# Spreading per-token factors over the partitions: a transpose of the stretched column in place of an fp32 matmul with the identity

## The chip, the cores and the metric

The kernel runs on one core of one Trainium2 chip, as one launch. The metric is the device time of that launch in microseconds. A profile is one execution, recorded with the start and length of every instruction. The engines are TensorE (PE; its weight loads are PEld), VectorE (DVE), ScalarE (ACT), GpSimd (POOL) and SyncE (SP, which issues most of the DMA transfers). Each runs its own queue in order; semaphores tie them together.

## The reference

A token sequence of 256 positions by 1024 features goes through two layers of a first block and one layer of a second, in fp32. What matters here is that every stage begins with, or contains, a norm: a factor per token that multiplies all features of that token.

```python
def rms_norm(x, g):
    x32 = x.astype(jnp.float32)
    y = x32 * lax.rsqrt(jnp.mean(x32 * x32, axis=-1, keepdims=True) + EPS)
    return (y * g.astype(jnp.float32)).astype(x.dtype)

for i in range(DEPTH):                     # first block, DEPTH = 2
    x = x + 0.5 * swiglu(rms_norm(x, g[0]), ...)
    h = rms_norm(x, g[1])
    m = even_mixer(h, ...) if i % 2 == 0 else mla_mixer(h, ...)
    x = x + m
    x = x + 0.5 * swiglu(rms_norm(x, g[2]), ...)
    x = x + per_layer_embedding(rms_norm(x, g[3]), p[i], ..., g[4])   # ends in a norm
# second block, one layer
u = rmsnorm(x, norm_mix) @ w_in            # attention, a state-space part, pooling
x = x + concatenate([y_attn, y_ssd, y_pool]) @ w_out
x = x + swiglu(rmsnorm(x, norm_ffn), ...)
return rmsnorm(x, norm_final)
```

The even mixer holds a gated recurrence whose output has a norm per token and head (4 heads). The state-space part needs, per head (6), the running sum of a decay along the tokens, both down the partitions and along the columns: `exp(a_cum[l] - a_cum[s])`; its output has a norm per token and group (2 groups).

## The kernel before

Activations lie feature-major: 128 features down the partitions, 256 tokens along the columns, eight such tiles for 1024 features. Weights stream in from HBM as pieces of 128 x 2048 and are split on chip into a high and a low part (`whi` by ACT at line 248, `wlo` by DVE at line 249), as are the activations (`hh` and `hl`, or `big`, or `o`). Each product of a 128 x 128 weight tile is three matmuls of 256 columns, high by high, high by low, low by high, which accumulate in a bank (`acc`, four of them). A second set of four banks (`aux`) takes everything small.

`fm` (line 319) runs a list of weight chunks over the eight (or 22) activation tiles; its evacuation multiplies by the factor per token `rb`. That factor is made beside the matmuls by `Stat`: `begin` (line 69) lets PE sum the squares into a column per half of the tokens, with the token on the partition, and DVE takes the reciprocal root; `finish` (line 88) then has to turn each column of 128 factors into a row that stands on all 128 partitions, since tokens lie along the columns in what it multiplies. The column is read with a stride of zero, as if it were 128 equal columns, and PE multiplies its transpose by the identity, into one half of an `aux` bank; ACT copies the bank to `rb` (line 99).

```python
for b in range(NB):                                   # NB = 2, line 92
    k.bcast(pb[:, b * P : (b + 1) * P], self.r[:, b : b + 1].to_broadcast([P, P]))
```

The same `bcast` (line 289) is used in the recurrence's output norm (line 808, eight times), in `states` of the state-space part (line 1293, two calls of six) and in `normed` (lines 1352 to 1354, six times; the middle one takes a column pair that was spread to 64 columns each, `kw`). Each goes through `mm` (line 162), the helper by which nearly all matmuls are issued, so the profile shows them under line 163, and they are told apart by their tiles: `ident` and `ny`, `ac` or `kw`.

The order on each engine is made by the framework's planner, which goes through the program with priorities and its own cost for every instruction and puts instructions that are ready into the queues. The kernel steers it: `behind(ins)` (line 165) holds what is issued inside it until `ins` has been placed, and `high_priority` lets DVE's and ACT's work of a norm go first. The ten calls of `finish` from within `fm` and the eight broadcasts of the recurrence's norm are behind a named matmul. The three calls through `now` (line 102: the two norms that close a layer embedding, and the last norm) and those of `states` and `normed` are not.

Where the kernel transposes data, as in `attend` (line 1119), in latent attention (`transposed`, line 936) and for the state-space inputs (line 1274), it uses `nc.tensor.transpose` with the same identity tile already.

Of the kernel before, what the change touches and what calls it, by code (L numbers as in the profile page):

```python
# [106 lines left out]
class Kern:  # L107
# [180 lines left out]

    def bcast(self, out, col, w=P):

        self.mm(out, col, self.ident)


    def sq_add(self, src, j, own=False):
# [1346 lines left out]
```

## Time and profile before

| | us |
|---|---|
| timed runs, median of 3 | 1368.15 |
| lowest and highest of them | 1366.81, 1370.12 |
| the profiled execution, its own time | 1364.73 |
| its span, first to last instruction | 1363.0 |
| PE busy | 1335.7 |
| DVE busy | 920.0 |
| ACT busy | 726.8 |

The span is what the views of the profile divide up; the profiled execution's own time is 1.7 us longer. A view by time merges neighbouring instructions of one kind on one engine into a row with a count; the second number is then the time from the first one's start to the last one's end. Matmuls overlap: each is listed with a length from its start until its last result, and the next starts long before that. The clock that the throttle granted to PE stands as a share of full speed (1.00 is 2.4 GHz, 0.50 is 1.2 GHz). A weight load and its matmul are two instructions (PEld and PE).

### The profile page before, as it was taken

What the parts mean: (1) busy time and instruction counts of PE and PEld (TensorE: products, weight loads), DVE (VectorE), ACT (ScalarE), POOL (GpSimd) and SP (SyncE); (2) the same over time, 40 slices, a digit from 0 to 9 for tenths busy, and PEclk for the clock granted to TensorE, in tenths of its full rate; (3) what the DMA queues carried; (4) which work ended last, traced back from release to release, by engine and by line L of the source; (5) the groups of instructions that cost most, each with busy time, mean ns of one, the idle gap of its engine ahead of it and who ended that gap; (6) DMA issues with size and microseconds to landing.
All of it is one profiled execution on the core that took longest, in us unless ns stands there. A gap on an engine that the chain in (4) does not pass through costs nothing.

```text
span 1363.0 us, 25969 instructions
## 1 busy us (share of the span) xinstructions
PE 1335.7 (98%) x10872; PEld 1304.9 (96%) x10872; DVE 920.0 (67%) x1527; ACT 726.8 (53%) x1110; POOL 78.3 (6%) x94
## 2 busy tenths in 40 slices
PE   8999999999999999999999899999998999999997
PEld 7999999999999999999999679999998988999997
DVE  6866657968666557866556767766558786766643
ACT  6554546646554456655445656544445665644442
POOL 3100010002000001000010002000001000200001
PEclk9999999999999999999999999999998999999998
DMA  9755555244555453555455323555554442555541
GB/s 323 244 185 183 171 201 173 90 174 168 200 188 203 160 203 138 200 190 188 166 194 193 108 90 132 184 188 188 180 185 156 155 149 100 181 190 187 185 158 60
DMA packets 34645, 235.50 MB, mean 173 GB/s; under 512 B 3984, under 2 KB 4496, under 8 KB 6880
## 3 DMA queue, kind: packets, MB, share of 16 engines
q1 hardware_dynamic: 32976, 230.24, 48.9%
q0 software_dynamic: 832, 2.47, 0.6%
q8 instruction: 85, 1.39, 0.4%
q10 hardware_dynamic: 720, 1.13, 0.2%
q14 instruction: 32, 0.26, 0.1%
HBM read 232.78 MB, written 1.05 MB: 172 GB/s over the span
## 4 chain that ended last, share of the span: by engine, by line
PE 75%; DVE 3%; ACT 2%; issue 1%; DVEq 0%; ACTq 0%
PE acc L163 70%; PE aux L163 5%; DVE wlo L249 1%; PE aux L1119 0%; ACT whi L248 0%; DVE big L1164 0%; DVE qs L950 0%; ACT at L1121 0%; DVE kv L950 0%; ACT ae L1111 0%; ACT big L938 0%; ACT big L1168 0%; DVE big L1486 0%; ACT gu L949 0%; PE aux L936 0%
## 5 line engine op out<-in xcount | busy, mean ns | idle before, releaser
L249 DVE TENSOR_TENSOR wlo<-wraw,whi 128x1024 fp32r<-128x1024 f32 (+1 forms) x440 | 530.8, 1220 | 271.8 <-ACT whi L248 179.8
L248 ACT ACTIVATE whi<-wraw 128x1024 fp32r<-128x1024 f32 (+1 forms) x440 | 451.1, 1047 | 329.0 <-PE acc L163 234.7
L163 PE MATMUL acc<-hh,whi 128*128 128x256 f32 x2192 | 335.0, 283 | 9.0 <-ACT whi L248 5.8
L163 PE MATMUL acc<-hl,whi 128*128 128x256 f32 x2192 | 333.9, 282 | 0.2 <-DVE hl L532 0.2
L163 PE MATMUL acc<-hh,wlo 128*128 128x256 f32 x2192 | 333.1, 282 | 0.7 <-DVE wlo L249 0.7
L163 PEld LDWEIGHTS acc<-hh,whi 128*128 128x128 f32 x2192 | 292.1, 190 | 9.7 <-ACT whi L248 5.8
L163 PEld LDWEIGHTS acc<-hh,wlo 128*128 128x128 f32 x2192 | 292.1, 189 | 1.5 <-DVE wlo L249 1.1
L163 PEld LDWEIGHTS acc<-hl,whi 128*128 128x128 f32 x2192 | 292.2, 189 | 0.4 <-DVE hl L532 0.4
L163 PE MATMUL acc<-big,whi 128*128 128x256 f32 x2032 | 276.1, 282 | 0.0
L163 PEld LDWEIGHTS acc<-big,whi 128*128 128x128 f32 x2032 | 259.7, 188 | 0.4 <-ACT big L259 0.2
L163 PE MATMUL acc<-big,wlo 128*128 128x256 f32 x1016 | 163.6, 282 | 0.0
L163 PEld LDWEIGHTS acc<-big,wlo 128*128 128x128 f32 x1016 | 138.9, 188 | 0.0
L307 POOL TENSOR_TENSOR sqa<-sqa,sq 128x256 f32<-128x256 f32 x72 | 64.0, 889 | 1148.1 <-ACT sq L306 1146.2
L418 DVE TENSOR_TENSOR gu<-acc,rb 128x512 f32<-128x512 f32 (+1 forms) x122 | 81.9, 678 | 56.3 <-PE acc L163 56.3
L262 ACT ACTIVATE hh<-x,cols 128x256 fp32r<-128x256 f32 x64 | 30.2, 503 | 85.2 <-DVE x L457 79.0
L259 ACT ACTIVATE big<-pr 128x256 fp32r<-128x256 f32 x114 | 46.0, 409 | 54.7 <-DVE pr L436 53.0
L434 ACT ACTIVATE sg<-gu 128x256 f32<-128x256 f32 x110 | 44.7, 411 | 37.4 <-DVE gu L418 37.4
L260 DVE TENSOR_TENSOR big<-pr,big 128x256 fp32r<-128x256 f32 x114 | 47.3, 420 | 20.5 <-ACT big L259 20.4
L436 DVE TENSOR_TENSOR pr<-sg,gu 128x256 f32<-128x256 f32 x110 | 45.3, 418 | 3.2 <-ACT sg L434 3.2
L263 DVE SCALAR_TENSOR_TENSOR hl<-x,cols,hh 128x256 fp32r<-128x256 f32 x64 | 37.8, 617 | 8.9 <-ACT hh L262 8.6
L163 PE MATMUL aux<-big 128*128 128x128 f32 (+5 forms) x260 | 39.3, 311 | 0.6 <-DVE big L672 0.6
L306 ACT ACTIVATE sq<-x 128x256 f32<-128x256 f32 x62 | 24.0, 405 | 24.5 <-DVE x L459 18.3
(294 smaller groups left out, 798.3 us busy)
## 6 DMA issues: line engine op xcount, KB each, us to landing
wraw<-wts SPq DMA_DIRECT2D x216, 1024.0 KB, 4.9
wraw<-wts SPq DMA_DIRECT2D x3, 512.0 KB, 8.3
x<-xT SPq DMA_DIRECT2D x3, 256.0 KB, 7.5
wraw<-wts SPq DMA_DIRECT2D x2, 256.0 KB, 3.9
big<-wsT POOLq DMA_DIRECT2D x1, 512.0 KB, 12.6
gu<-pT ACTq DMA_DIRECT2D x2, 256.0 KB, 2.9
out<-big SPq DMA_DIRECT2D x2, 256.0 KB, 2.2
out<-big ACTq DMA_DIRECT2D x2, 256.0 KB, 2.5
```

What stands on the lines that cost most here:

```text
L163: return self.nc.tensor.matmul(out, l, r, start=start, stop=stop, skip_group_check=True).ins
L248: nc.scalar.activation(hi[:, i], s, AF.Copy)
L249: nc.vector.tensor_tensor(lo[:, i], s, hi[:, i].bitcast(FT), op=OP.subtract)
L259: a = nc.scalar.activation(hi, src, AF.Copy)
L260: b = nc.vector.tensor_tensor(lo, src, hi.bitcast(FT), op=OP.subtract)
L262: a = nc.scalar.activation(hi, src, AF.Copy, scale=scale)
L263: b = nc.vector.scalar_tensor_tensor(lo, src, scale, hi.bitcast(FT), op0=OP.mult, op1=OP.subtract)
L306: nc.scalar.activation(q, src, AF.Square)
L307: self.mark = nc.gpsimd.tensor_tensor(self.sq[0], self.sq[0], q, op=OP.add).ins
L418: self.nc.vector.tensor_tensor(out.rearrange("p (u t) -> p u t", u=n), ps.rearrange("p (u t) -> p u t", u=n), rb.unsqueeze(1).to_broadcast ...
L434: self.mark = nc.scalar.activation(sg, gu[:, :T], AF.Silu).ins
L436: nc.vector.tensor_tensor(pr, sg, gu[:, T:], op=OP.mult)
```

## The change

`bcast` issues a PE transpose of the stretched column instead of a matmul of the stretched column by the identity. Operands, output bank and places of call stay; what the callers do stays too.

```diff
     def bcast(self, out, col, w=P):
 
-        self.mm(out, col, self.ident)
+        self.nc.tensor.transpose(out, col, self.ident)
```

## Rows read from the trace of the kernel before

**Rows 1.** Page, part 1: busy us, share of span, instructions by engine

```profile
PE 1335.7 (98%) x10872; PEld 1304.9 (96%) x10872; DVE 920.0 (67%) x1527; ACT 726.8 (53%) x1110; POOL 78.3 (6%) x94
```

**Rows 2.** Page, part 4: the chain that ended last, by line

```profile
PE acc L163 70%; PE aux L163 5%; DVE wlo L249 1%; PE aux L1119 0%; ACT whi L248 0%; DVE big L1164 0%; DVE qs L950 0%; ACT at L1121 0%; DVE kv L950 0%; ACT ae L1111 0%; ACT big L938 0%; ACT big L1168 0%; DVE big L1486 0%; ACT gu L949 0%; PE aux L936 0%
```

**Rows 3.** Stretches: length; PE, PEld, DVE, ACT, POOL busy (count); clock, DMA share, GB/s

```profile
530.00:560.00 30.00, 28.23 (x234) 27.83 (x234) 25.44 (x55) 19.10 (x33) 0.00 (x0) 1.00 0.35 116
740.00:830.00 90.00, 84.63 (x530) 70.43 (x529) 63.10 (x165) 54.55 (x106) 0.00 (x0) 1.00 0.31 106
830.00:1030.00 200.00, 200.00 (x1699) 199.93 (x1698) 130.69 (x191) 100.84 (x149) 12.59 (x14) 1.00 0.54 185
1030.00:1060.00 30.00, 26.10 (x197) 25.34 (x196) 25.77 (x50) 20.38 (x38) 5.33 (x5) 0.89 0.31 106
sum 1363.00, PE 1335.65 PEld 1304.91 DVE 920.03 ACT 726.81 POOL 78.27; mean PE 111.30 PEld 108.74 DVE 76.67 ACT 60.57 POOL 6.52
```

**Rows 4.** Instructions reading the identity: ns min/median/max; who waited (us, times)

```profile
L163 PE MATMUL aux<-ident,ny x76: 270/275/580, 26.5 to 1355.8; 128*128 128x128 f32 x76
L1119 PE MATMUL aux<-ident,ae x42: 270/273/332, 790.8 to 1145.6; 128*128 128x128 f32 x42
L163 PE MATMUL aux<-ident,ac x24: 270/275/376, 1103.1 to 1114.7; 128*128 128x128 f32 x24
L163 PE MATMUL aux<-ident,kw x4: 275/275/275, 1141.9 to 1142.7; 128*128 128x128 f32 x4
  ACT rb L99: 7.0, 7
```

**Rows 5.** PE by time, states: start, first start to last end, instruction, count

```profile
1103.12 1.50 PE L163 MATMUL aux<-ident,ac 128*128 128x128 f32 x12
1104.37 0.49 PE L163 MATMUL acc<-hl,whi 128*128 128x256 f32 x2
1104.69 0.28 PE L163 MATMUL acc<-hh,wlo 128*128 128x256 f32 x1
```

**Rows 6.** PE by time, inside the gate and up matmuls of an FFN

```profile
518.81 1.11 PE L163 MATMUL acc<-hl,whi 128*128 128x256 f32 x8
519.76 1.11 PE L163 MATMUL acc<-hh,wlo 128*128 128x256 f32 x8
```

**Rows 7.** PE by time, transposes of attend among the output projection's matmuls

```profile
798.40 0.49 PE L1119 MATMUL aux<-ident,ae 128*128 128x128 f32 x3
798.65 0.48 PE L163 MATMUL acc<-o,whi 128*128 128x256 f32 x2
798.96 0.28 PE L163 MATMUL acc<-o,wlo 128*128 128x256 f32 x1
```

**Rows 8.** PE by time, behind the second post norm

```profile
1051.63 0.41 PE L163 MATMUL acc<-hh,whi 128*128 128x256 f32 x1
1051.84 0.41 PE L163 MATMUL acc<-hl,whi 128*128 128x256 f32 x1
```

**Rows 9.** The closing norm by time; in brackets idle before, and its releaser

```profile
1354.96 1.22 PE L163 MATMUL aux<-ident,ny 128*128 128x128 f32 x4 [1.21 <-DVE ny L286]
1356.22 0.42 DVE L1486 TENSOR_TENSOR big<-x,aux 128x256 f32<-128x256 f32 x1 [1.31 <-PE aux L163]
```

**Rows 10.** Stretches with the granted clock (after POOL), columns as in group 3

```profile
754.00:784.00 30.00, 25.59 (x134) 19.92 (x133) 23.93 (x61) 20.04 (x33) 0.00 (x0) 1.00 0.31 105
1047.00:1050.00 3.00, 1.42 (x7) 1.13 (x8) 2.21 (x6) 1.27 (x4) 0.00 (x0) 0.55 0.95 319
1050.00:1054.00 4.00, 4.00 (x21) 4.00 (x20) 3.88 (x10) 2.70 (x8) 0.00 (x0) 0.50 0.06 23
```

**Rows 11.** PE and DVE by time, the recurrence's output norm

```profile
296.19 1.95 PE L163 MATMUL aux<-ident,ny 128*128 128x128 f32 x16
297.89 0.48 PE L163 MATMUL acc<-big,whi 128*128 128x256 f32 x2
299.02 0.74 DVE L263 SCALAR_TENSOR_TENSOR big<-big,cols 128x512 fp32r<-128x512 f32 x1
```

## Prediction

> **What bounds the kernel now.** I read the engine totals first, then the chain of work that ended last, then the busy time by stretch, and only then the instructions that the change replaces. The totals show TensorE (PE) busy for 1335.7 of 1363.0 us, VectorE for 67% and ScalarE for 53% [rows 1]. A busy PE is not proof of a bound, so the chain comes second: its largest item by far is PE's accumulating matmuls, 70% of the span, with another 5% on PE's matmuls into the small `aux` banks, which is where the changed ones write [rows 2]. The stretches show where that holds. From 830 to 1030 us (one of the FFNs, which fill most of the span) PE is busy for all of the 200 us. It has holes only where a mixer or a norm makes it wait: 90 - 84.63 = 5.4 us in 740 to 830 (latent attention), 1.8 us around 530 to 560 and 3.9 us in 1030 to 1060 (the two norms behind the layer embeddings) [rows 3]. Over the whole span PE waits 1363.0 - 1335.65 = 27 us, a good part of it before its first matmul and after its last. So an instruction taken out of PE's queue moves everything behind it forward, unless a wait of a fixed kind follows; there are few.
>
> **What is removed.** `bcast` stands in 52 places: two in each of 13 calls of `finish` (26), eight in the gated recurrence's output norm, twelve in the state-space part's `states`, six in its `normed`. The trace shows each as two matmuls with a weight load each: 76 + 24 + 4 = 104 = 2 x 52 [rows 4]. I call one of the two a pass. The change puts one transpose in the place of each pair; the 42 transposes that the kernel has already in `attend` (14 calls of three) are one instruction each in the trace [rows 4]. So 52 matmuls and 52 weight loads go, and 52 change their kind.
>
> **What a pass costs.** Its duration (median 275 ns [rows 4]) is no price, since matmuls overlap; the price is by how much it pushes the next start. In dense FFN work eight 256-column matmuls start in 519.76 - 518.81 = 0.95 us, 0.119 us each [rows 6]. Twelve passes and two such matmuls lie between the starts at 1103.12 and 1104.69: 1.57 - 2 x 0.119 = 1.33 us, so 0.111 us a pass, 0.222 us a `bcast` [rows 5].
>
> **What a transpose costs.** No row of before shows a transpose of a stretched column; the nearest are the transposes of `attend` in the middle of dense work. Three of them and two matmuls lie between 798.40 and 798.96: 0.56 - 0.24 = 0.32 us, 0.107 us each [rows 7]. That is one pass, within what two decimals allow. Bounds: not below half a pass, since the same 128 columns still have to be loaded and streamed (I take 0.056 us), and not above the two passes that it replaces (0.222 us), which is a rival below. I take 0.11 us, by the row that does the same thing on the same engine with the same shape; the stretched read as weights is no new thing, since the passes read the same column in the same way.
>
> The Trainium skill's page "TensorE: Matmul & The Clock Gate", section Terms, says that a transpose mode makes fp32 four times as fast. Taken against the pair, that would be an estimate of 0.222 / 4 = 0.056 us a transpose and a gain of 52 x 0.167 = 8.7 us. The row at 798.40 disagrees: against a pair the transpose is twice as fast, not four times.
>
> **The sum.** At the full clock a `bcast` falls from 0.222 to 0.11 us. Of the 52, 50 run there: 50 x 0.112 = 5.6 us. The last two stand in the closing norm, in a stretch at half the clock, where a start takes 1051.84 - 1051.63 = 0.21 us [rows 8]: 2 x 0.21 = 0.4 us. There PE waits on nothing else and VectorE waits for the last of the four passes [rows 9], so this is kept whole. Together 6.0 us.
>
> What of it lies on the path? In the ten `finish` calls within dense work, PE runs on before and behind, so 0.22 us each moves all later work; that ScalarE sat idle for 7.0 us in seven cases until the broadcast was there [rows 4] costs nothing either way. In the three closing or post norms PE has no other work and the chain runs through the broadcast: shorter by the same two starts. In the recurrence's norm eight pairs take 297.89 - 296.19 = 1.70 us, and 24 matmuls of the output projection cover the scaling behind them (24 x 0.119 = 2.86 us, to 300.75). The low half of the first scaled operand is ready at 299.02 + 0.74 = 299.76 [rows 11]. PE now comes to it 0.9 us sooner, while the operand, which hangs on the first four pairs, comes only 0.45 us sooner: the cover shrinks from 1.0 to about 0.5 us and holds. If it did not, the wait would be under 0.5 us. `states` and `normed` stand between other matmuls, in the same way. The work of DVE and ACT is untouched, and weights come through a ring of buffers that PE itself frees, so a sooner PE also calls them sooner: DVE is busy for 130.69 us of 200 in an FFN stretch [rows 3], so it has room.
>
> **The time.** The profiled execution took 1364.73 us, 1.7 us more than its span of 1363.0. By the sum it would take 1364.7 - 6.0 = 1358.7. The median of the three timed runs is 1368.15 (1366.81 to 1370.12), 3.4 us above the profiled one, and I predict in its terms: 1368.15 - 6.0 = 1362.1 us.
>
> **Rivals.**
> (a) *Absorbed.* The waits that exist (5.4 us in latent attention, 3.9 and 1.8 us around the post norms) are ended by DVE or ACT [rows 3]; if these, and not PE, set the pace in the stages around them, what is saved ahead comes back as a longer wait. Against it: these engines get their work from PE's results, so they start sooner as well. Half kept gives 1368.15 - 3.0 = 1365.1 us.
> (b) *The clock.* The granted clock is full but for short stretches: 0.55 and 0.50 in 1047 to 1054, behind a post norm in which PE was busy for 1.42 us of 3, and at the end [rows 10]. In that stretch a matmul took 0.21 us of room, where dense work gives 0.119 [rows 6, 8], so five dense microseconds there lose about 5 x (1 - 0.119 / 0.21) = 2.2 us. If transposes counted for less with the clock than matmuls do, the post norm at 536 us would lose the clock too: 1362.1 + 2.2 = 1364.3. Against it: through 754 to 784 us, with some sixty transposes, matmuls between, and waits, the clock stayed at 1.00 [rows 10]. The skill's same page, section "Part 4: PE-mode transpose", says that the full clock does not set in for transposes, as they do not count as activity in the same way. By that rule this change could cost such a stretch; the row speaks against it where transposes stand in bunches among matmuls.
> (c) *It does not do what it says.* The transpose of a stretched fp32 column could take as long as two passes. Then nothing moves: 1368.1 us. For it: no row of that operand. Against it: every fp32 transpose here is one instruction and one pass [rows 4, 7].
> (d) *Slower.* The kernel is laid out by a planner that goes by its own cost for each instruction. A cheaper broadcast lets it put other work first in the places that are not pinned: the mixers, where PE's queue already interleaves attention and projections. PE runs its queue in order, so one instruction put ahead of its operand holds all behind it. If the idle time in the three stretches that have holes (5.4 + 1.8 + 3.9 = 11.1 us) doubled, the time would be 1368.15 - 6.0 + 11.1 = 1373.2. It decides from 6.0 + 2.7 = 8.7 us of new waits on. Against it: 28 of the 52 broadcasts (ten `finish` calls and the recurrence's norm) are pinned behind a named matmul.
>
> **How the numbers follow.** About 0.2% (2.7 us) is what a measurement of this kernel can tell from no change, so faster means under 1365.4. Chances: forecast 0.70, (a) 0.11, (b) 0.08, (c) 0.06, (d) 0.05. Faster: the forecast, (b) and half of (a), less 0.08 for the spread of single executions (3.3 us between the three runs): 0.75. Same: (c), the other half of (a) and that spread: 0.20. Slower: 0.05. The range runs from 1358.0 (a transpose at its lower bound gains 52 x 0.166 = 8.6, so 1359.5, and the 1.3 us by which the lowest run lies under the median) to 1367.0 (half kept, 1365.1, and the 2.0 us by which the highest run lies above it); it leaves out (c) and (d).
>
> **What would show it.** One transpose instead of each pair, 10820 matmuls in all, weight loads of those 52 at another length than the passes'; the next matmul 0.11 us later for each; DVE and ACT as busy as before; the clock row as before. A `bcast` that still pushes the next start by 0.22 us would prove (c), new or longer waits on PE in the mixers (a) or (d), another stretch at half clock (b).

## The result, and the profile after

The changed kernel takes 1356.55 us (median of four runs, 1355.18 to 1358.94); the kernel before, run beside it, takes 1367.48 (1366.74 to 1370.12). The ratio is 0.9928, with a 95% interval of 0.9907 to 0.9949. The kernel is faster by 9.8 us by the ratio, with the interval running from 7.0 to 12.7 us. The forecast was 6.0 us. The direction is right, the size is not: the time lies 1.45 us below the low end of the range.

The profiled execution of the changed kernel took 1355.69 us with a span of 1354.0. Part 1 of its page (busy us, share of the span, instructions of each engine), and the chain that ended last, by line:

```profile
PE 1327.2 (98%) x10820; PEld 1298.7 (96%) x10820; DVE 921.4 (68%) x1527; ACT 727.0 (54%) x1110; POOL 78.6 (6%) x94
...
PE acc L163 71%; PE aux L163 4%; DVE wlo L249 1%; PE aux L291 0%; PE aux L1119 0%; DVE big L1164 0%; ACT whi L248 0%; DVE qs L950 0%; DVE kv L950 0%; DVE big L503 0%; ACT ae L1111 0%; ACT big L938 0%; ACT big L1168 0%; DVE big L1486 0%; ACT gu L949 0%
```

Against [rows 1] there are 52 matmuls and 52 weight loads fewer, and PE is busy for 8.5 us less; DVE and ACT have the same counts and nearly the same times. The chain is as in [rows 2]. What reads the identity, by instruction (ns least, median, most; then first and last start), once for PE and once for its weight loads, answers to [rows 4]:

```profile
L291 PE MATMUL aux<-ident,ny x38: 270/272/453, 26.6 to 1346.9; 128*128 128x128 f32 x38
...
L291 PE MATMUL aux<-ident,ac x12: 270/272/323, 1100.8 to 1110.0; 128*128 128x128 f32 x12
...
L291 PE MATMUL aux<-ident,kw x2: 273/273/273, 1134.7 to 1135.1; 128*128 128x128 f32 x2
...
  ACT rb L99: 5.2, 7
```

```profile
L291 PEld LDWEIGHTS aux<-ident,ny x38: 132/134/217, 26.5 to 1346.8; 128*128 128x128 f32 x38
```

One transpose stands in the place of each pair of passes (38 + 12 + 2 = 52), the weight load takes 134 ns, and ACT waits 5.2 us for the broadcast where it waited 7.0. By time, the first bunch of `states` (start, length to the last end, instruction, count) answers to [rows 5], and the closing norm to [rows 9]:

```profile
1100.81 0.82 PE L291 MATMUL aux<-ident,ac 128*128 128x128 f32 x6
1101.38 0.37 PE L163 MATMUL acc<-hl,whi 128*128 128x256 f32 x1
1101.59 0.88 PE L163 MATMUL acc<-hh,wlo 128*128 128x256 f32 x6
...
1346.72 0.43 PE L291 MATMUL aux<-ident,ny 128*128 128x128 f32 x2 [1.21 <-DVE ny L286]
...
1347.19 0.42 DVE L1486 TENSOR_TENSOR big<-x,aux 128x256 f32<-128x256 f32 x1 [0.53 <-PE aux L291]
```

Six transposes push the next start by 1101.38 - 1100.81 = 0.57 us, about 0.10 each; the passes, counted in the same way, took 1104.37 - 1103.12 = 1.25 us for twelve, 0.104 each [rows 5]. So a transpose takes the room of one pass. In the closing norm VectorE waits 0.53 us, not 1.31, but part of that is the clock (see below).

### Where the 9 us lie

I cut both spans at the first broadcast of each norm or `states` and compared the pieces. The two profiled executions differ by 1363.02 - 1353.98 = 9.04 us (the table is worked out from the starts in the two traces; pieces with about 0.1 us of difference or less are left out):

| piece | before, us | after, us | difference |
|---|---|---|---|
| first FFN | 184.14 | 181.53 | -2.61 |
| even mixer, to the recurrence's norm | 85.54 | 85.29 | -0.25 |
| the recurrence's norm and projection | 33.64 | 32.77 | -0.87 |
| second FFN and the layer embedding behind it | 187.59, 18.91 | 187.31, 18.68 | -0.51 |
| around the first post norm | 22.30 | 21.73 | -0.57 |
| third FFN | 180.47 | 181.40 | +0.93 |
| latent attention | 109.85 | 110.91 | +1.06 |
| fourth FFN | 181.88 | 182.88 | +1.00 |
| around the second post norm | 24.12 | 23.67 | -0.45 |
| last mixer | 109.64 | 103.76 | -5.88 |
| last FFN | 174.35 | 174.12 | -0.23 |
| closing norm | 8.06 | 7.26 | -0.80 |

The quiet pieces show what the prediction said: 0.23 to 0.28 us for each two transposes, 0.87 where eight stand. Three things are not in it: 5.88 us in the last mixer, where 20 broadcasts should give 2.2; pieces that became longer; and 2.61 us in the first FFN, where 0.22 were due. The experiments are about these. The first, third and fourth FFN and latent attention together come to -2.61 + 0.93 + 1.00 + 1.06 = +0.38 us: what varies there between single executions nearly cancels in this pair of profiles.

### The profile page after: what moved, and what is told of

Its sections match the earlier page's. It is cut to its first block, busy times and chain, and to the rows that moved or that the text cites. A ratio compares the mean times of both kernels' runs of the same rounds, so it can differ in the third digit from the quotient of the medians.

```text
span 1354.0 us, 25869 instructions
## 1 busy us (share of the span) xinstructions
PE 1327.2 (98%) x10820; PEld 1298.7 (96%) x10820; DVE 921.4 (68%) x1527; ACT 727.0 (54%) x1110; POOL 78.6 (6%) x94
## 3 DMA queue, kind: packets, MB, share of 16 engines
HBM read 232.78 MB, written 1.05 MB: 173 GB/s over the span
## 4 chain that ended last, share of the span: by engine, by line
PE 75%; DVE 4%; ACT 2%; issue 1%; DVEq 0%; ACTq 0%
PE acc L163 71%; PE aux L163 4%; DVE wlo L249 1%; PE aux L291 0%; PE aux L1119 0%; DVE big L1164 0%; ACT whi L248 0%; DVE qs L950 0%; DVE kv L950 0%; DVE big L503 0%; ACT ae L1111 0%; ACT big L938 0%; ACT big L1168 0%; DVE big L1486 0%; ACT gu L949 0%
```

## The experiments

In all of them "the last mixer" is the piece of the table, from the first broadcast of its opening `finish` to the first of the next FFN's. Its length comes from one profiled execution of each kernel, and is steady: 109.64 and 109.63 us in two executions of the kernel before, 103.76 and 103.94 in two of the one after.

### The order and the instruction, apart

The changed program differs from the one before in more than the 52 places. By the order of the starts in the two traces, with the broadcasts left out, 75 of PE's 10768 other matmuls stand at another place, all of them between 1100 and 1149 us of the kernel before, and that is in the last mixer. Of VectorE's 1527 instructions 21 and of ScalarE's 1110 15 stand elsewhere, most of them there too; GpSimd's and SyncE's order is the same.

So the planner, given a cheaper broadcast, laid the last mixer out anew. Two kernels take the order and the instruction apart. `order_before` lets the planner see the matmuls of before and turns the 52 pairs into transposes after planning; `order_after` lets it see transposes and runs them as matmuls. In their traces PE starts its matmuls in the order of the kernel before and of the kernel after.

```diff
     def bcast(self, out, col, w=P):
-        self.mm(out, col, self.ident)
+        self.casts.append(self.mm(out, col, self.ident))
...
         k.run()
+    names = {i.name for i in k.casts}
+    for f in nc.m.functions:
+        for block in f.blocks:
+            for n, i in enumerate(block.instructions):
+                if i.name in names:
+                    block.instructions[n] = copy.replace(i, is_transpose=True)
```

`order_after` does the reverse: `nc.tensor.transpose` in `bcast`, and `is_transpose=False` afterwards. `after_again` is the changed kernel once more, and `rest_only` gives transposes to 34 of the 52 alone (`finish` and the recurrence's norm), planned as such.

> All 52 broadcasts run as transposes, but the planner laid the program out as if they were matmuls: every engine's order is that of the kernel before. Order theory (the transposes give 52 x 0.11 = 6.0 us, and the planner's other order in the state-space mixer gives the remaining 3.6 us): about 1367.5 - 6.0 = 1361.5 us, and the stretch of the last mixer (from the first broadcast of states to the end of its output projection) keeps its 31 us but for 18 x 0.11 = 2.0 us. Cheap-transpose theory (a transpose takes less room than a pass, so the whole 9 to 11 us come from it): 1357 to 1358 us, as the changed kernel.

> All 52 broadcasts run as pairs of fp32 matmul passes, but the planner laid the program out as if they were transposes: every engine's order is that of the changed kernel. Order theory: about 1367.5 - 3.6 = 1363.9 us, though nothing is transposed. Cheap-transpose theory: 1367.5 us, no change.

> The changed kernel again, on the chip of the two crossed kernels. If its 10.9 us are order plus transposes, it lies at 1367.5 - 6.0 - 3.6 = 1357.9 us or lower by the spread of dense stretches; if they are spread between executions, it comes out near the kernel with the order of before, at 1361.5 us.

> Transposes only in finish and in the recurrence's norm (34 of 52); the 18 of states and normed stay fp32 matmuls. Transposes alone: 34 x 0.11 + 0.2 = 3.9 us, 1363.6 us. If the planner's order in the last mixer moves by itself when work ahead of it gets shorter, it departs from that by a few us in either direction, and the mixer's stretch shows it; if the order there changes only with the broadcasts in it, 1363.6 us holds.

Measured beside the kernel before (1365.2 us, 29 runs), with the length of the last mixer:

| kernel | order | broadcast | us | ratio (95%) | last mixer, us |
|---|---|---|---|---|---|
| before | old | pass pairs | 1365.2 | 1 | 109.64 |
| order_before | old | transposes | 1361.21 | 0.9968 (0.9953 to 0.9982) | 108.60 |
| order_after | new | pass pairs | 1362.91 | 0.9984 (0.9969 to 0.9999) | 106.23 |
| after_again | new | transposes | 1357.0 | 0.994 (0.992 to 0.996) | 103.94 |
| rest_only | a third | both | 1359.65 | 0.9967 (0.995 to 0.9985) | 107.52 |

The stretch of each kernel's last mixer: length, busy time of PE, PEld, DVE, ACT and POOL with counts, clock, DMA share, GB/s. Before:

```profile
1070.96:1180.61 109.65, 109.24 (x845) 100.90 (x844) 84.27 (x202) 69.83 (x126) 7.12 (x7) 1.00 0.44 153
```

order_before:

```profile
1069.39:1177.99 108.60, 107.45 (x825) 98.78 (x823) 84.19 (x202) 69.89 (x126) 7.11 (x7) 1.00 0.45 154
```

order_after:

```profile
1075.25:1181.48 106.23, 105.85 (x845) 99.90 (x844) 84.62 (x202) 70.13 (x126) 7.12 (x7) 1.00 0.45 158
```

After:

```profile
1068.85:1172.61 103.76, 103.39 (x825) 97.44 (x824) 84.61 (x202) 70.00 (x126) 7.11 (x7) 1.00 0.46 162
```

The new order alone takes 109.65 - 106.23 = 3.4 us out of the last mixer, with the same instructions, and PE has no more idle time in it (0.38 us against 0.41): the gain is in PE's busy time. By the timed runs the order alone gains 2.2 us with an interval of 0.1 to 4.2, which holds the 3.4 but would not show them by itself. The transposes take 106.23 - 103.76 = 2.5 us more in the new order, but only 109.65 - 108.60 = 1.05 us in the old one, where PE's idle time grew from 0.41 to 1.15 us. What PE waited for there, in `order_before`:

```profile
PE aux L1119 <- DVE ae L1115: 0.6, 1, 0.6
```

```profile
1139.57 0.36 PE L163 MATMUL acc<-big,whi 128*128 128x256 f32 x1
1140.55 0.33 PE L1119 MATMUL aux<-ident,ae 128*128 128x128 f32 x1 [0.61 <-DVE ae L1115]
```

The first row (line waited for: us, times, longest) is PE's wait in 1130 to 1150, the others the place. A transpose of `attend` comes up sooner than its softmax, and PE stands: this is rival (a), in the old order and at this place. From one start to the next 0.98 us pass here, so the place costs more than the 0.61 us that count as idle. In the kernel after, other work stands here, and its last mixer has no such wait.

By summing the time from each start to the next over the last mixer, the 40 passes hold PE for 4.23 us in the kernel before and the 20 transposes for 1.91 in the kernel after: 0.116 us saved a broadcast. The crossed kernels give the same (4.24 us for the passes in `order_after`, 1.91 for the transposes in `order_before`), so this price does not hang on the order. It is that of the prediction (0.112).

### What the new order does

The same sums, by kind of matmul, show what the order alone gained (before against `order_after`): the score matmuls of 64 rows fall from 3.78 to 2.77 us, `attend`'s transposes from 2.14 to 1.48, the products with `at` from 4.62 to 4.10, the pooling's from 2.88 to 2.40. That is 2.7 of the 3.4 us. The instructions are the same; each holds PE for less. In the starts a matmul behind one of another height, width or kind often comes 0.2 to 0.3 us after it, where equal dense ones follow in 0.119, so an order with fewer such changes should be shorter. The third pair of attention heads shows how. PE by time, before:

```profile
1134.15 0.48 PE L163 MATMUL aux<-big 64*128 64x128 f32 x2
1134.56 0.33 PE L1119 MATMUL aux<-ident,ae 128*128 128x128 f32 x1
1134.82 0.70 PE L163 MATMUL aux<-big 64*128 64x256 f32 x2
1135.45 0.44 PE L1119 MATMUL aux<-ident,ae 128*128 128x128 f32 x2
...
1137.26 0.92 PE L163 MATMUL aux<-big 64*128 64x128 f32 x4
1138.11 0.39 PE L163 MATMUL acc<-o,whi 128*128 128x256 f32 x1
```

After:

```profile
1130.70 0.93 PE L163 MATMUL aux<-big 64*128 64x128 f32 x8
1131.56 0.39 PE L163 MATMUL acc<-o,wlo 128*128 128x256 f32 x1
```

Before, the first head's scores (four instructions, two products of two passes) are broken up by another head's transposes: 1134.15 to 1135.45 is 1.30 us for five instructions, and the second head's four take 1138.11 - 1137.26 = 0.85 us. After, all eight stand together and take 1131.56 - 1130.70 = 0.86 us. Their starts in the trace lie 13, 200, 13, 99, 13, 205, 13 and 306 ns apart: the second head of a pair has its features on the other 64 partitions, so its matmul starts 13 ns behind the first's. A head alone (the second head before: 213, 112, 218 and 306 ns) leaves half of PE's rows unused and takes as long as two.

To test this by itself I wrote the order by hand: the scores of two heads are issued alternately. `pair_hyb_before` does it in the last mixer of the kernel before; `pair_mla_after` in latent attention of the kernel after, whose heads also have a product of 64 rows; `pair_both_after` in both. Beside them, `hybrid_only` gives transposes to `states` and `normed` alone (18 of 52).

```diff
+    def scores(self, heads):
+        n = len(heads[0][1])
+        for i in range(n):
+            for u in range(2):
+                for ps, pairs in heads:
+                    q, k = pairs[i]
+                    if u == 0:
+                        self.mm(ps[:, :P], q[:, :P], k[:, :P], i == 0, False)
+                    else:
+                        self.mm(ps[:, P : P + T], q[:, P:], k, False, i == n - 1)
```

> Transposes only in states and normed (18 of 52); finish and the recurrence's norm stay fp32 matmuls. The transposes alone give 18 x 0.116 = 2.1 us in the last mixer (from the first broadcast of its finish to that of the next FFN's: 109.6 us before, 103.8 after). Order theory: the planner again finds an order of its own there, and the stretch ends between 108.6 (the old order, with waits for attend's softmax where the passes were) and 103.8 us, by whether the third pair of heads has its 64-row score matmuls side by side. If the gain were the transposes' alone, the stretch would be 107.5 us in any order. First FFN (first to second broadcast): 184.1 us as before if its slower step comes from the passes in front of it, 181.5 to 182.8 if not.

> The kernel before, with its fp32 matmul broadcasts, but in the last mixer the score matmuls of the two heads of a pair are issued in turn, so that 64-row matmuls on the two halves of the array stand side by side. Side-by-side theory: these 24 instructions go from 3.78 us to 3 x 0.86 = 2.6 us (two of the three pairs have it already), the third pair's 1.9 us become 0.86, so about 1.0 us of the 109.6 us of that stretch go, more or less what else the planner moves. If the order's gain has another cause, the 24 instructions take 3.78 us as before.

> The changed kernel, with the score matmuls of two heads issued in turn in latent attention, where all eight heads' 64-row rotary parts run alone now: 8 x 0.85 us = 6.8 us of PE's time. Side-by-side theory: 4 x 0.86 = 3.4 us, a gain of 3.4 us over the changed kernel (about 1353 to 1354 us), unless waits for the softmax eat it: the stretch has 5.4 us of PE waits already, and two heads' scores early hold two banks. If side by side is not what counts, no change from 1357.

> The changed kernel with the scores of two heads issued in turn in both mixers. In the last mixer all three pairs stand side by side already, so that half should bring nothing by itself: the same as the kernel with latent attention's pairs alone, within 1 us, if the planner's order stays as good as it was; a loss of up to 3 us there if it does not.

Measured beside the kernel before (1367.93 us, 19 runs):

| kernel | us | ratio (95%) | last mixer, us | latent attention, us |
|---|---|---|---|---|
| hybrid_only | 1363.24 | 0.9968 (0.9957 to 0.9979) | 105.70 | 111.10 |
| pair_hyb_before | 1365.78 | 0.9992 (0.9982 to 1.0003) | 108.75 | 109.65 |
| pair_mla_after | 1355.65 | 0.9911 (0.9893 to 0.9929) | 103.84 | 110.01 |
| pair_both_after | 1355.62 | 0.9917 (0.9902 to 0.9932) | 104.51 | 109.99 |

Pairing by hand in the old order takes 0.9 us out of the last mixer (the 64-row scores fall from 3.78 to 3.15 us, the rest by the places around them). That shows the mechanism, and that it is about a quarter of the order's 3.4 us; over the whole kernel it is too small to be resolved. The rest lies with the other kinds of matmul named above; it was seen in the sums and not tried alone, so its cause is argued and not shown. `pair_both_after` is no better in the last mixer than the planner's own new order, which has the pairs already.

`hybrid_only` and `rest_only` plan still other orders: 105.70 us with 18 transposes in the last mixer, 107.52 us with two. In `rest_only` those two, at the head of the piece, are worth 0.2 us by themselves, and 2.1 went. The planner's layout of this stage changes with few of its costs, and its length moves by microseconds.

In latent attention the pairs halve the eight heads' scores, from 6.80 to 3.42 us, as was expected (4 x 0.86). Yet the piece, 110.01 us, is hardly shorter than in the kernel after (110.91 and 109.72 in two profiles). PE now waits 1.9 us for the first softmax, and behind that wait the granted clock fell to 0.50 for a while (0.85 over 787 to 794 us). Summed from start to start the scores come to 5.43 us, the number that the expectation of `pair_mla_late` goes by, but that sum holds the wait, which follows a score. In `pair_mla_after`, the wait (line waited for: us, times, longest) and the stretch:

```profile
PE aux L1126 <- DVE ae L1122: 2.3, 2, 1.9
```

```profile
787.00:794.00 7.00, 4.72 (x23) 2.98 (x21) 6.20 (x24) 5.78 (x16) 0.00 (x0) 0.85 0.42 150
```

The first exponential starts 50.7 us into the piece, against 50.8 in the kernel after, so the softmax is ready no sooner, and PE has run out of other work before it. So `pair_mla_late` leaves heads 0 and 1 single and pairs the others (against `pair_mla_after`):

```diff
-            if h % 2 == 0:
+            if h < 2:
+                score(h)
+                self.scores([scored[h]])
+            elif h % 2 == 0:
                 score(h)
                 score(h + 1)
                 self.scores([scored[h], scored[h + 1]])
```

### The first FFN, and the spread of single executions

Three more kernels are about the 2.61 us of the first FFN. Its piece took 184.14 us in the profiles of before, `order_after` and `hybrid_only`, which have passes in its `finish`, and 181.53 in most kernels with transposes there, so the passes might have put the matmuls behind them out of step. `first_only` is the kernel before with transposes in the first `finish` alone; `all_but_first` is the kernel after with passes there alone; both keep their kernel's order. `before_again` is the kernel before, unchanged, as a run of its own.

```diff
     def bcast(self, out, col, w=P):
-        self.mm(out, col, self.ident)
+        self.done += 1; (self.nc.tensor.transpose if self.done <= 2 else self.mm)(out, col, self.ident)
```

> Transposes in the first finish alone (two broadcasts, in the first FFN); every engine's order is that of the kernel before. So far the stretch from the first to the second broadcast took 184.1 us in three of four profiles with fp32 matmuls there, and 181.5 or 182.8 us in all with transposes. Step theory (the two passes there leave the dense matmuls behind them on a longer step, 0.120 us in place of 0.117): 181.5 to 182.8 us there and a gain of 0.2 + 1.3 to 2.4 us in all. Chance theory (the step is drawn anew in each execution, whatever stands in front): a gain of 0.2 us, and a stretch of any of the three lengths.

> The changed kernel with the first finish's two broadcasts as fp32 matmuls again; every engine's order is that of the changed kernel. Step theory: 184.1 us from the first to the second broadcast, and a loss of 1.5 to 2.6 us against the changed kernel (about 1359). Chance theory: a loss of 0.2 us.

> The kernel before, another profiled execution of it: which of its stretches keep their length. Step theory: the first FFN at 184.1 us again. Both: the last mixer (from the first broadcast of its finish to that of the next FFN's) at 109.6 us, since its order is fixed, and the dense stretches of the other FFNs within about 2.5 us of the first profile's.

> The changed kernel, with the scores of two heads issued in turn in latent attention from the third head on; the first two stand alone as before. The version with all pairs gained 1.4 us of PE's time in the 64-row matmuls (6.80 to 5.43 us) and lost it again to a wait of 1.9 us for the first softmax, after which the clock fell. Without that wait: 3 x 0.34 = 1.0 us or, if all three pairs stand wholly side by side, 3 x 0.85 = 2.5 us under the changed kernel, so 1354.5 to 1356.

Measured beside the kernel before (1368.09 us, 23 runs):

| kernel | us | ratio (95%) | first FFN, us | last mixer, us |
|---|---|---|---|---|
| first_only | 1365.11 | 0.9978 (0.9968 to 0.9988) | 181.54 | 109.67 |
| all_but_first | 1357.15 | 0.9923 (0.9911 to 0.9936) | 181.77 | 103.74 |
| before_again | 1368.09 | 0.9995 (0.9983 to 1.0007) | 181.77 | 109.63 |
| pair_mla_late | 1354.11 | 0.9898 (0.9885 to 0.991) | 181.54 | 103.69 |

The kernel before itself shows 181.77 us in its second profile, and `all_but_first` shows 181.77 with passes: 0.24 more than with transposes, which is their direct price. So passes do not force the longer stretch. What differs is the step of dense matmuls. PE by time at the same place, first in the first profile of before, then in `before_again`:

```profile
60.43 1.12 PE L163 MATMUL acc<-hh,wlo 128*128 128x256 f32 x8
61.39 1.12 PE L163 MATMUL acc<-hh,whi 128*128 128x256 f32 x8
```

```profile
60.64 1.10 PE L163 MATMUL acc<-hh,whi 128*128 128x256 f32 x8
61.58 1.10 PE L163 MATMUL acc<-hl,whi 128*128 128x256 f32 x8
```

Eight matmuls start in 0.96 us in the one and in 0.94 in the other. Over all of the FFN's gate and up matmuls (about 990 starts) the mean step is 119.8 ns in the one and 117.5 ns in the other, and 118.7 in `order_before`; the down matmuls behind them take 118.7 ns in every profile. The same instructions in the same order run at either step. The other FFNs do the same, independently (the third 180.2 to 181.6 us, the fourth 181.7 to 183.1, the second 187.3 to 190.1): the 0.93 and 1.00 us by which the third and fourth grew are a step of 118.6 or 118.7 ns in place of 117.5. Another source of the spread is the clock. In `before_again` there are two stretches at less than full clock that [rows 3] doesn't have:

```profile
536.00:542.00 6.00, 4.45 (x22) 4.25 (x23) 5.82 (x15) 3.88 (x10) 0.00 (x0) 0.72 0.37 153
745.00:756.00 11.00, 11.00 (x61) 9.64 (x60) 5.27 (x20) 4.99 (x9) 0.00 (x0) 0.84 0.40 139
```

and in the profile of the kernel after one, in the same stage:

```profile
744.80:748.40 3.60, 3.60 (x9) 2.82 (x10) 1.54 (x10) 0.34 (x1) 0.00 (x0) 0.53 0.59 250
```

They are at the lower level, 1.2 GHz, for a part of the window shown. Such stretches came up behind the first post norm (about 536 us) in 4 of 6 profiles with passes there and 4 of 8 with transposes, and at the start of latent attention (745 to 750 us) in 4 of 6 and 5 of 8. These profiles show no link to the kind of broadcast.

The closing norm varies in the same way. Its first 2 to 3 us, in this order: before, `before_again`, after, `pair_mla_late` (columns as in [rows 3]):

```profile
1354.96:1358.20 3.24, 1.22 (x4) 0.93 (x4) 1.53 (x5) 0.39 (x1) 1.06 (x2) 0.50 0.00 0
```

```profile
1358.58:1360.50 1.92, 0.71 (x4) 0.52 (x4) 0.72 (x2) 0.38 (x1) 0.26 (x1) 1.00 0.00 0
```

```profile
1346.72:1348.70 1.98, 0.43 (x2) 0.19 (x2) 1.06 (x3) 0.38 (x1) 0.59 (x1) 1.00 0.00 0
```

```profile
1345.20:1347.30 2.10, 0.69 (x2) 0.28 (x2) 0.93 (x3) 0.38 (x1) 0.46 (x1) 0.50 0.00 0
```

At the granted clock 0.50 the piece takes 8.06 us with passes (before) and 7.51 with transposes (`pair_mla_late`); at 1.00 it takes 7.54 (`before_again`) and 7.26 (after). So the 0.80 us of the table compare passes at 1.2 GHz with transposes at 2.4 GHz; at one level of the clock the transposes are worth 0.55 or 0.28 us.

One thing stays open. `first_only` is 2.2 permille faster than before, 3.0 us with an interval of 1.6 to 4.4, where its own transposes account for 0.2. In the profiles the 184.14 us of the first FFN came in three of six kernels with passes in the first `finish`, and in none of eight with transposes (one of these had 182.75). Over all five FFNs of the 14 profiles, the step of 119.8 or 119.9 ns came in 4 of 30 with passes at their head and in none of 40 with transposes; in the profile of before it begins right behind the passes, where the starts ahead of them lie 115 to 122 ns apart and those behind exactly 120. It may be that passes make the longer step more frequent; but four cases are few, and `all_but_first`, with passes there, lost nothing that can be seen against the kernel after. No timed run shows its steps, so this stays open.

`pair_mla_late` is the fastest kernel of the study, 1354.11 us (1353.14 to 1354.41). The interval of its ratio lies just below that of `all_but_first`, run beside it, which is the kernel after but for two broadcasts. Of the 3.0 us between their medians the profiles account for 1.1 (0.2 for the two broadcasts, 0.9 in latent attention, 109.55 to 108.67). Its wait for the first softmax is smaller (line waited for: us, times, longest):

```profile
PE aux L1129 <- DVE ae L1125: 1.3, 2, 0.9
```

Without that wait the eight heads' scores hold PE for 4.26 us instead of 6.80 (two at 0.85, three pairs at 0.86), and latent attention takes 108.67 us in its profile, with a stretch at the 1.2 GHz level in it, where the kernel after took 109.72 (without one) and 110.91 (with one).

## Why the prediction fell short

**What bounds the kernel** held. PE is busy for 98% of the span as before, the chain is the same, and outside the last mixer, where PE's order is the same, each broadcast moved all later work forward by its saving.

**The price of a pass and of a transpose** held: 0.116 us saved a broadcast in the last mixer against 0.112, 0.23 to 0.28 a `finish` against 0.22 (the table). The estimate that was drawn from the Trainium skill's page "TensorE: Matmul & The Clock Gate", section Terms (a gain of 8.7 us) is contradicted by the 0.10 us that a transpose takes at 1100.81: it is half of a pair, not a quarter. That the result, 9.8 us, lies near 8.7 is chance. `order_before`, with all 52 transposes and the old order, gained 4.4 us.

**The recurrence's norm** held: the piece fell by 0.87 us, the 8 x 0.11 of the prediction, and PE has no new wait there.

**The closing norm** was mis-sized a little. It was put at 0.4 us at half the clock [rows 8, 9], and at that level it gives 0.55: of the four passes the first holds PE for 373 ns, not 210, before the next starts, and of the two transposes the first holds 267 (`pair_mla_late`). The kernel after showed 0.80 because its closing norm ran at the full clock, where 0.28 would be due against passes at the same clock. Which level that norm gets differs between executions of the kernel before (0.50 in one profile, 1.00 in the other), so the rest of the 0.80 is luck of the two profiles.

**The order** is the step of the prediction that failed. The sum held the planner's new order at nothing. Rival (d) named the planner and the right place (the mixers, which are not pinned), but with one sign: I looked for what an order is worth in PE's idle time alone, as new waits. The runs showed a gain of 3.4 us in the last mixer from the order alone, out of PE's busy time. The warning was in the reading itself: a busy PE need not be at its peak. I had listed the 64-row matmuls and never asked whether they stand next to their partners. A gain of that size as a second arm of (d) would have put the low end below the result, and added to the sum it would have given 1368.15 - 9.4 = 1358.7 us, inside the stated range; the 2.2 us that remain are within the spread of the timed runs.

**Rival (a)** came true only in the old order, with 1.3 of the 2.3 us lost in the last mixer there (`order_before`; 0.7 of it as idle time), and not in the kernel after, whose order has other work at that place. **Rival (b)** finds no support: stretches at half the clock came in 8 of 12 places with passes and 9 of 16 with transposes. The rule of the Trainium skill's page "TensorE: Matmul & The Clock Gate", section "Part 4: PE-mode transpose", that the full clock does not set in for transposes, shows no effect here, where the transposes stand among matmuls. (The stretch from 754 to 784 us, which the prediction sets against (b), holds 54 transposes, not sixty; its clock of 1.00 stands.) **Rival (c)** fell at once: one instruction for each pair, 0.10 us each.

**The anchor** was sound: 1368.15 us against 1367.48 beside the changed kernel and 1365.2, 1367.9 and 1368.1 in the later runs. The range was too narrow as well: its own terms give 1358.2 to 1367.1 us (stated as 1358.0 to 1367.0), while single executions of the kernel before run from 1361 to 1371 us in the later runs, and I had taken the spread from three. The profiles show two things that vary so, the FFNs' step and the stretches at half the clock.

The sum with what was measured: 50 x 0.116 = 5.8 us, the closing norm 0.28 to 0.55 at one level of the clock, the order 3.4, together 9.5 to 9.8 us, against 9.8 (7.0 to 12.7) by the ratio, and 8.2 and 10.5 by the other two comparisons of (nearly) the same kernel (`after_again`, `all_but_first`). So good an agreement is in part luck, since the intervals are 4 to 6 us wide.

## What to carry to other kernels

Where a planner lays out the instructions, an edit that makes one instruction cheaper is two changes: the instruction, and the new order of everything near it. Price the second with both signs, compare the queues of both programs first, and measure them apart by planning with the one and running the other. Before trusting a 98% busy TensorE, list its matmuls of half height or half width and look at whether those on different halves stand next to each other; if not, issue them alternately, except at the head of a chain that something waits for.

## What the runs showed of the hardware

Two fp32 matmuls of 64 rows on different halves of the partitions start 13 ns apart in the last mixer of the kernel after and 5 to 8 ns apart in latent attention of `pair_mla_after`, where two on the same half start 112 to 218 ns apart (the second head at 1137.26, before). The Trainium skill's page "TensorE: Matmul & The Clock Gate", section "Part 3: Packing small matmuls — row/col tiling", says that matmuls on different row groups run at the same time; the trace agrees, with 5 to 13 ns from start to start where the page has about 4.

A stream of 128 x 256 matmuls, each with its weight load, can run at one of several steady mean steps: the gate and up matmuls of the first FFN kept 119.8, 118.7 or 117.5 ns over about 990 starts, in executions of the same matmuls in the same order. It is worth 2.4 us in the first FFN, and I know no cause.

An fp32 transpose of 128 x 128 takes half the room of an fp32 matmul of that size: the matmul shows as two passes of 0.11 us each, the transpose as one instruction of 0.10 to 0.11. At half the granted clock, in the closing norm, two transposes start 267 ns apart where at the full clock they start 160 ns apart (`pair_mla_late`, after).
